# First embedding gate: the norm's root is made by token and spread by a diagonal product, and two sums into the stream run on GpSimd

## The chip, the cores and the metric

The kernel runs on one core of one Trainium2 chip. A core has TensorE (PE, with its weight loads as PEld), VectorE (DVE), ScalarE (ACT), GpSimd (POOL) and SyncE (SP), which here issues the DMAs of the weights. The metric is the device time of one execution in microseconds; the median of three runs of the kernel before is 1048.97 us (1047.62 to 1049.02).

## The reference, cut to what matters

Two decoder layers run over 256 tokens of width 1024 in float32. Each layer is a half-step SwiGLU, a token mixer, a second half-step SwiGLU, and a gated input embedding:

```
for i in range(2):
    h = h + 0.5 * swiglu(rms_norm(h, g_ffn1[i]), ...)
    h = h + mixer_i(rms_norm(h, g_mix[i]), ...)
    h = h + 0.5 * swiglu(rms_norm(h, g_ffn2[i]), ...)
    gate = sigmoid(rms_norm(h, g_ple[i]) @ ple_w_gate[i])
    h = h + gate * (p[i] @ ple_w_proj[i])
# rms_norm(x, g) = x * rsqrt(mean(x * x) + 1e-6) * g
```

The change touches the last two lines of layer 0 only. Layer 1 has a gate of its own (`ple_last`), which is left as it is.

## The kernel before, in words

The residual stream `h` is kept transposed in SBUF: 128 partitions by 8 blocks of the width by 256 tokens. A norm is split in two. `Norm.chunk(dp)` takes two blocks of `h` as soon as they are final: ACT writes the high part of h times the gain (L374), DVE the low part (L376), ACT the squares (L382), and GpSimd adds the squares up (L384) and folds them to `ss` at the fourth chunk (L388). The factor of each token, one over the root of its mean square, is applied behind the matrix product that the norm feeds. A float32 weight is used as two parts: ACT casts the high part `whi` (L86), DVE subtracts it for the low part `wlo` (L87); each block of weights needs three products (L234 to L236), or a wide one and a narrow one (L255, L248) in the feed-forward.

In the gate of layer 0 (`ple`), PE first makes the projection of p (two PSUM tiles of two banks each), then the gate's product in four steps `dp`, each of 48 products into one PSUM tile of the pool `psb`, which has four buffers. After the first half of step 0 the function calls `norm.spread()` (L1087): a product of `ss` with a constant matrix (L394) sums over the partitions and leaves the mean of each token on all 128 partitions, 128x256; DVE adds epsilon (L396) and takes the inverse root in ten instructions of 128x256 (`rsqrt`, L354 and three times L356 to L358). Each step then has its tail: DVE multiplies the gate by `r`, ACT takes the sigmoid (L1090), DVE multiplies by the projection and adds the result into `h` (the instructions of DVE are all recorded under the helper's line, L349), and `after.chunk(dp)` makes the two blocks of input for the next layer's first feed-forward.

That feed-forward (`ffn`) starts with the blocks of width 0 to 5 of the gate and the up product (the wide products of a unit of weights first, then its narrow ones), then blocks 6 and 7; so its fifth block, the first of chunk 2, is needed after eight wide products.

The order on each engine is set by the framework's planner: it lists instructions by their place in the program and puts the first one that its own timing calls ready into the engine's queue. The engine then runs that queue strictly in order. `order(...)` and `steady(...)` pin an instruction behind its engine's previous one of the program while they are switched on; in `ple` both are off, in the feed-forward `steady` is on. SP's weight loads are pinned always.

Two forms that the change brings to this place exist elsewhere in the kernel: `by_token` (L401), where `ss` is the stationary operand and one column of the constant matrix the moving one, so that the means stand on the partitions, 128x2, and a spread by a diagonal matrix in the opening of the kernel (`roots`, L1181 to L1195).

Of the kernel before, what the change touches and what calls it, by code (L numbers as in the profile page):

```python
# [9 lines left out]
F32 = mybir.dt.float32  # L10
# [3 lines left out]
ALU = mybir.AluOpType  # L14
AX = mybir.AxisListType

P = 128
S = 256
# [133 lines left out]
def trunk(ctx: ExitStack, tc: tile.TileContext, a: dict, out: bass.AP):  # L152
    nc = tc.nc
# [4 lines left out]
    stat = ctx.enter_context(tc.tile_pool(name="stat", bufs=2))  # L158
# [5 lines left out]
    def pa():  # L164
        return psa.tile([P, 1024], F32, name="pa", tag="pa")

    def pb():
        return psb.tile([P, 512], F32, name="pb", tag="pb")
# [62 lines left out]
    def mm_w(ps, wt, cols, x, k, start, stop):  # L231

        hi, lo = wt[0][:, cols], wt[1][:, cols]
        steady(nc.tensor.matmul(ps, lhsT=hi, rhs=x[:, k, 0, :], start=start, stop=False, skip_group_check=True))  # L234
        steady(nc.tensor.matmul(ps, lhsT=hi, rhs=x[:, k, 1, :], start=False, stop=False, skip_group_check=True))  # L235
        return steady(nc.tensor.matmul(ps, lhsT=lo, rhs=x[:, k, 0, :], start=False, stop=stop, skip_group_check=True))  # L236
# [32 lines left out]
    start = ExitStack()  # L269
# [40 lines left out]
    ident = const.tile([P, P], F32, name="ident")  # L310
# [3 lines left out]
    ones = const.tile([P, P], F32, name="ones")  # L314
# [33 lines left out]
    def tt_op(o, x, y, op):  # L348
        return nc.vector.tensor_tensor(o, x, y, op=op)  # L349

    def rsqrt(x, n, o):

        t = stat.tile([P, n], F32, name=f"rs_t{n}", tag=f"rs_t{n}", bufs=1)
        order(nc.vector.tensor_scalar(o.bitcast(I32), x.bitcast(I32), -0.5, 1597463007.0, op0=ALU.mult, op1=ALU.add))  # L354
        for _ in range(3):
            order(nc.vector.scalar_tensor_tensor(t, o, -0.5, o, op0=ALU.mult, op1=ALU.mult))  # L356
            order(nc.vector.tensor_tensor(t, t, x, op=ALU.mult))
            order(nc.vector.scalar_tensor_tensor(o, t, 1.5, o, op0=ALU.add, op1=ALU.mult))  # L358

    h = const.tile([P, KD, S], F32, name="h")  # L360

    class Norm:
# [38 lines left out]
        def by_token(self):  # L401

            ss = self.ss
            ms = pb()
            for tt in range(2):
                nc.tensor.matmul(
                    ms[:, tt : tt + 1], lhsT=ss[:, tt * P : (tt + 1) * P], rhs=mean_d[:, 0:1], start=True, stop=True
                )
            x = stat.tile([P, 2], F32, name="mst", tag="mst", bufs=1)
            nc.vector.tensor_scalar(x, ms[:, :2], EPS, None, op0=ALU.add)  # L410
            return x

    def two(r):
        return r.unsqueeze(1).broadcast_to([P, 2, S])
# [652 lines left out]
    def ple(norm, pt, after, pool):  # L1067
        x = norm.x
        wt = w.get()
        pr = []  # L1070
        for q in range(2):
            ps = pa().rearrange("p (b t) -> p b t", b=4)
            for b in range(4):
                for k in range(2):
                    c = (4 * q + b) * P
                    mm_w(ps[:, b, :], wt(k), slice(c, c + P), pt, k, start=(b % 2 == 0 and k == 0), stop=(k == 1))
            pr.append(ps)
        r = None
        for dp in range(4):
            wt = w.get()  # L1080
            gp = pb().rearrange("p (b t) -> p b t", b=2)
            for kh in range(2):
                for b in range(2):
                    for k in range(kh * 4, kh * 4 + 4):
                        mm_w(gp[:, b, :], wt(k), slice(b * P, (b + 1) * P), x, k, start=(k == 0 and b == 0), stop=(k == KD - 1))
                if r is None:
                    r = norm.spread()  # L1087
            gt = pool.tile([P, 2, S], F32, name="gt", tag="gt")
            tt_op(gt, gp, two(r), ALU.mult)
            nc.scalar.activation(gt, gt, AF.Sigmoid)  # L1090
            tt_op(gt, gt, pr[dp // 2][:, 2 * (dp % 2) : 2 * (dp % 2) + 2, :], ALU.mult)
            tt_op(h[:, 2 * dp : 2 * dp + 2, :], h[:, 2 * dp : 2 * dp + 2, :], gt, ALU.add)
            after.chunk(dp)

    def ple_last(norm, pt, pool):
# [44 lines left out]
    norm = Norm(0, 0)  # L1140
# [14 lines left out]
    sums, mean, rt = (const.tile([P, 2], F32, name=n) for n in ("row_sums", "row_mean", "row_r"))  # L1155
# [64 lines left out]
    for i in range(2):  # L1220
        nxt = Norm(1, i)
        with tc.tile_pool(name=f"ffn1_{i}", bufs=2, reuse_waits="tile") as pool:
            if i == 0:
                ffn(norm, nxt, pool, {0: lambda *_: small_loads(), 4: lambda *marks: later(pool, *marks)}, opened)
            else:
                ffn(norm, nxt, pool)
        norm = nxt
        with tc.tile_pool(name=f"mix_{i}", bufs=2, reuse_waits="tile") as pool:
            lazy = Lazy(Norm, 2, i)
            (mla if i == 0 else fox)(norm, lazy, pool)  # L1230
            norm = lazy.norm
        pt = p_parts(i)
        nxt = Norm(3, i)
        with tc.tile_pool(name=f"ffn2_{i}", bufs=2, reuse_waits="tile") as pool:
            ffn(norm, nxt, pool)
            norm = nxt
            if i == 0:
                lazy = Lazy(Norm, 0, 1)
                ple(norm, pt, lazy, pool)
                norm = lazy.norm  # L1240
            else:
                ple_last(norm, pt, pool)
# [41 lines left out]
```

## Time and profile before

| | |
|---|---|
| median of three runs | 1048.97 us (1047.62 to 1049.02) |
| the profiled execution | 1049.13 us |
| its span in the profile | 1047.4 us (1.7 us lie around it) |
| mean granted clock of TensorE | 0.997 of full speed |
| PE, DVE, ACT, POOL busy | 99%, 74%, 57%, 7% of the span |

The profile gives for each engine the time in which it was busy, and for each wait the instruction that released it. A clock of 1.00 means 2.4 GHz, of 0.50 means 1.2 GHz. The gate of layer 0 lies from 489 us (the projection) over 494.6 us (the gate's first product) to 518.1 us (the next feed-forward's first product). Times "at" a moment are counted from the start of the span.

### The profile page before, as it was taken

The page shows a single profiled execution, that of the slowest core. Times are in us where ns is not written, and L with a number is a line of the kernel's source. Part 1 is how long each engine was busy: PE and PEld are TensorE (multiplying, and loading weights), DVE is VectorE, ACT ScalarE, POOL GpSimd, SP SyncE. Part 2 cuts the span into 40 slices and gives each one's busy share as a digit, 9 for nine tenths or more (in the row PEclk, how much of TensorE's full clock was granted, in tenths as well). Part 3 has the DMA queues.
Part 4 walks back from the last instruction along what each step waited for, and adds up shares of the span by engine and source line. Part 5 has one row for each costly group of instructions (what it writes and reads, how often), then busy time and mean ns, then how long its engine had stood idle before and what let it go on. Part 6 is the DMA issues. An engine that isn't in the chain of part 4 may idle for free.

```text
span 1047.4 us, 16326 instructions
## 1 busy us (share of the span) xinstructions
PE 1034.1 (99%) x6380; PEld 918.5 (88%) x6380; DVE 777.6 (74%) x1369; ACT 600.0 (57%) x903; POOL 77.9 (7%) x99
## 2 busy tenths in 40 slices
PE   8999999999999999999999999999999999999998
PEld 7888888987898888889888888889998988888886
DVE  5888766679979776666987776658888797776664
ACT  6665544568766655455656555535655666554552
POOL 0000000233110000001110000011000200000010
PEclk9999999999999999999999999999999999999999
DMA  7765555524336656556537565554743267555541
GB/s 243 242 226 183 185 181 172 181 93 170 106 107 201 214 188 191 183 185 206 170 126 240 188 201 174 188 154 141 227 135 113 95 197 227 182 185 191 181 161 41
DMA packets 171105, 182.60 MB, mean 174 GB/s; under 512 B 6094, under 2 KB 164372, under 8 KB 171028
## 3 DMA queue, kind: packets, MB, share of 16 engines
q1 hardware_dynamic: 170452, 181.03, 53.7%
q8 instruction: 50, 0.82, 0.3%
q10 hardware_dynamic: 576, 0.53, 0.1%
q14 instruction: 27, 0.22, 0.1%
HBM read 180.50 MB, written 1.05 MB: 173 GB/s over the span
## 4 chain that ended last, share of the span: by engine, by line
PE 94%; DVE 3%; DMA 1%; POOL 1%; ACT 0%; issue 0%; ACTq 0%; DVEq 0%
PE pa L255 46%; PE pa L248 23%; PE pa L264 3%; PE pa L266 3%; PE pa L265 3%; PE pa L234 2%; PE pa L236 2%; PE pa L235 2%; DVE wlo L87 1%; PE pb L612 1%; PE pb L519 1%; PE pb L559 1%; PE pb L547 1%; PE pb L518 1%; DMA xn<-in_x_dram 1%; PE pb L266 1%
## 5 line engine op out<-in xcount | busy, mean ns | idle before, releaser
L87 DVE TENSOR_TENSOR wlo<-raw,whi 128x1024 fp32r<-128x1024 f32 (+2 forms) x351 | 418.5, 1223 | 170.9 <-PE pa L248 71.9
L86 ACT CAST whi<-raw 128x1024 fp32r<-128x1024 f32 (+2 forms) x351 | 351.0, 1016 | 247.0 <-PE pa L255 175.9
L255 PE MATMUL pa<-xa,whi 128*128 128x512 f32 x1408 | 343.9, 395 | 1.9 <-DVE xa L376 1.8
L255 PEld LDWEIGHTS pa<-xa,whi 128*128 128x128 f32 x1408 | 258.7, 189 | 54.1 <-DVE xa L376 3.1
L248 PEld LDWEIGHTS pa<-xa,wlo 128*128 128x128 f32 x1408 | 179.1, 189 | 8.7
L248 PE MATMUL pa<-xa,wlo 128*128 128x256 f32 x1408 | 180.6, 279 | 0.0
L255 PE MATMUL pa<-hid,whi 128*128 128x512 f32 x704 | 169.2, 392 | 0.0
L255 PEld LDWEIGHTS pa<-hid,whi 128*128 128x128 f32 x704 | 128.8, 188 | 25.2
L384 POOL TENSOR_TENSOR sq<-sq 128x512 f32<-128x512 f32 x21 | 37.8, 1800 | 826.9 <-ACT sq L382 813.4
L248 PEld LDWEIGHTS pa<-hid,wlo 128*128 128x128 f32 x704 | 88.3, 188 | 4.0
L248 PE MATMUL pa<-hid,wlo 128*128 128x256 f32 x704 | 89.1, 278 | 0.0
L264 PE MATMUL pa<-whi,xa 128*128 128x256 f32 (+3 forms) x192 | 59.0, 307 | 0.0
L266 PE MATMUL pa<-whi,xa 128*128 128x256 f32 (+3 forms) x192 | 57.6, 300 | 0.0
L265 PE MATMUL pa<-wlo,xa 128*128 128x256 f32 (+3 forms) x192 | 57.2, 298 | 0.0
L234 PE MATMUL pa<-xa,whi 128*128 128x256 f32 x184 | 54.2, 295 | 0.0
L349 DVE TENSOR_TENSOR hid<-hf,hid 128x512 fp32r<-128x512 f32 x44 | 30.4, 692 | 29.0 <-ACT hid L442 29.0
L236 PE MATMUL pa<-xa,wlo 128*128 128x256 f32 x184 | 51.9, 283 | 0.0
L235 PE MATMUL pa<-xa,whi 128*128 128x256 f32 x184 | 51.9, 282 | 0.0
L432 ACT COPY gt<-pa 128x512 f32<-128x512 f32 x44 | 25.8, 586 | 39.1 <-PE pa L248 39.0
L432 ACT COPY hf<-pa 128x512 f32<-128x512 f32 x44 | 25.7, 584 | 28.1 <-PE pa L248 28.1
L438 ACT ACTIVATE gt<-gt 128x512 f32<-128x512 f32 x44 | 27.7, 629 | 19.4 <-DVE gt L349 19.3
L264 PEld LDWEIGHTS pa<-whi,xa 128*128 128x128 f32 x192 | 36.1, 188 | 1.4 <-issue 0.5
(281 smaller groups left out, 1215.1 us busy)
## 6 DMA issues: line engine op xcount, KB each, us to landing
raw<-in_ffn_w_in_dram SPq DMA_DIRECT2D x86, 1024.0 KB, 5.1
raw<-in_ffn_w_out_dram SPq DMA_DIRECT2D x32, 1024.0 KB, 5.2
raw<-in_ffn_w_out_dram SPq DMA_DIRECT2D x16, 768.0 KB, 4.5
raw<-in_ple_w_gate_dram SPq DMA_DIRECT2D x8, 1024.0 KB, 5.8
raw<-in_fox_w_in_dram SPq DMA_DIRECT2D x8, 1024.0 KB, 6.5
raw<-in_mla_w_o_dram SPq DMA_DIRECT2D x4, 1024.0 KB, 5.6
raw<-in_fox_w_o_dram SPq DMA_DIRECT2D x4, 1024.0 KB
raw<-in_mla_w_in_dram SPq DMA_DIRECT2D x3, 1024.0 KB, 6.7
```

The costliest lines, as they stand in the source:

```text
L86: self.order(self.nc.scalar.copy(h, whole))
L87: self.order(self.nc.vector.tensor_tensor(low, whole, h.bitcast(F32), op=ALU.subtract))
L234: steady(nc.tensor.matmul(ps, lhsT=hi, rhs=x[:, k, 0, :], start=start, stop=False, skip_group_check=True))
L235: steady(nc.tensor.matmul(ps, lhsT=hi, rhs=x[:, k, 1, :], start=False, stop=False, skip_group_check=True))
L236: return steady(nc.tensor.matmul(ps, lhsT=lo, rhs=x[:, k, 0, :], start=False, stop=stop, skip_group_check=True))
L248: nc.tensor.matmul(ps[:, 1, :], lhsT=wt(k)[1][:, cols], rhs=x[:, at + k, 0, :], start=False, stop=(k == last), skip_group_check=True,)
L255: nc.tensor.matmul(ps, lhsT=wt(k)[0][:, cols], rhs=x[:, at + k], start=(k == first), stop=False, skip_group_check=True)
L264: steady(nc.tensor.matmul(ps, lhsT=x[:, k, 0, t], rhs=wt[0], start=start, stop=False, skip_group_check=True))
L265: steady(nc.tensor.matmul(ps, lhsT=x[:, k, 0, t], rhs=wt[1], start=False, stop=False, skip_group_check=True))
L266: steady(nc.tensor.matmul(ps, lhsT=x[:, k, 1, t], rhs=wt[0], start=False, stop=stop, skip_group_check=True))
L384: nc.gpsimd.tensor_tensor(sq, sq, self.acc, op=ALU.add)
L432: nc.scalar.copy(o, ps[:, :, 0, :])
```

## The change

`spread_small` takes the place of `spread` in the gate of layer 0. It takes the means by token, the root on 128x2, puts the two columns of roots on the diagonal of two 128x128 matrices, and multiplies a matrix of ones with them, which leaves on all 128 partitions the factor of each token; ACT copies it out of PSUM. Beside that, the sums into `h` of steps 0 and 1 are issued on GpSimd instead of DVE.

```diff
+        def spread_small(self):
+
+            x = self.by_token()
+            rt = stat.tile([P, 2], F32, name="rt", tag="rt", bufs=1)
+            rsqrt(x, 2, rt)
+            diag = stat.tile([P, S], F32, name="ms", tag="ms", bufs=1)
+            for tt in range(2):
+                nc.vector.tensor_scalar(diag[:, tt * P : (tt + 1) * P], ident, rt[:, tt : tt + 1], None, op0=ALU.mult)
+            rp = pb()
+            nc.tensor.matmul(rp[:, :S], lhsT=ones, rhs=diag, start=True, stop=True)
+            r = stat.tile([P, S], F32, name="r", tag="r")
+            nc.scalar.copy(r, rp[:, :S])
+            return r
...
                 if r is None:
-                    r = norm.spread()
+                    r = norm.spread_small()
...
-            tt_op(h[:, 2 * dp : 2 * dp + 2, :], h[:, 2 * dp : 2 * dp + 2, :], gt, ALU.add)
+            hc = h[:, 2 * dp : 2 * dp + 2, :]
+            if dp < 2:
+                nc.gpsimd.tensor_tensor(hc, hc, gt, op=ALU.add)
+            else:
+                tt_op(hc, hc, gt, ALU.add)
```

## Rows read from the trace of the kernel before

**Rows 1.** The page, part 1: busy time, share and instructions of each engine.
```profile
PE 1034.1 (99%) x6380; PEld 918.5 (88%) x6380; DVE 777.6 (74%) x1369; ACT 600.0 (57%) x903; POOL 77.9 (7%) x99
```
**Rows 2.** Waits of PE in the whole span: us in total, times, longest.
```profile
PE pa L255 <- DVE xa L376: 1.8, 1, 1.8
...
PE pb L406 <- POOL ss L388: 1.2, 1, 1.2
...
PE pb L394 <- POOL ss L388: 0.3, 1, 0.3
```
**Rows 3.** Windows: PE, PEld, DVE, ACT, POOL busy; then granted clock, DMA share, GB/s.
```profile
498.00:507.00 9.00, 9.00 (x76) 8.95 (x76) 8.72 (x16) 2.63 (x4) 0.00 (x0) 1.00 0.57 180
507.00:514.00 7.00, 7.00 (x61) 7.00 (x61) 6.21 (x10) 6.47 (x10) 0.00 (x0) 1.00 0.68 220
514.00:522.00 8.00, 6.16 (x46) 5.47 (x44) 8.00 (x13) 6.32 (x11) 1.69 (x2) 1.00 0.41 132
522.00:530.00 8.00, 8.00 (x39) 7.11 (x40) 5.54 (x7) 3.27 (x5) 4.35 (x3) 0.79 0.41 132
```
**Rows 4.** Timeline of PE through the gate: start, us, instructions, idle before and releaser.
```profile
497.81 0.70 PE L394 MATMUL pb<-ss,mean_d 128*128 128x256 f32 x2 [0.34 <-POOL ss L388]
498.16 0.47 PE L234 MATMUL pb<-xa,whi 128*128 128x256 f32 x1
...
518.14 2.00 PE L255 MATMUL pa<-xa,whi 128*128 128x512 f32 x8
521.98 1.93 PE L255 MATMUL pa<-xa,whi 128*128 128x512 f32 x4 [1.84 <-DVE xa L376]
```
**Rows 5.** Timeline of DVE through the gate.
```profile
498.77 0.41 DVE L396 TENSOR_SCALAR ms<-pb 128x256 f32<-128x256 f32 x1
...
502.73 1.22 DVE L87 TENSOR_TENSOR wlo<-raw,whi 128x1024 fp32r<-128x1024 f32 x1
...
505.23 0.42 DVE L358 SCALAR_TENSOR_TENSOR r<-rs_t,r 128x256 f32<-128x256 f32 x1
...
510.00 1.28 DVE L349 TENSOR_TENSOR gt<-gt,pa 128x512 f32<-128x512 f32 x2 [0.72 <-ACT gt L1090]
...
515.13 0.68 DVE L349 TENSOR_TENSOR gt<-pb,r 128x512 f32<-128x512 f32 x1
...
521.45 0.87 DVE L376 SCALAR_TENSOR_TENSOR xa<-h,gvec,xa 128x256 fp32r<-128x256 f32 x2
```
**Rows 6.** Timeline of DVE in the opening: first and last of thirteen instructions in a row.
```profile
24.73 0.16 DVE L1184 TENSOR_SCALAR row_mean<-row_sums 128x2 f32<-128x2 f32 x1
...
26.96 0.48 DVE L1189 TENSOR_SCALAR ms<-ident,row_r 128x128 f32<-128x128 f32 x2
```
**Rows 7.** Timeline of PE in the opening and in the first mixer.
```profile
28.45 0.59 PE L1192 MATMUL pb<-ms,ones 128*128 128x256 f32 x2
...
209.11 0.50 PE L406 MATMUL pb<-mean_d,ss 128*128 128x1 f32 x4
...
210.22 0.50 PE L264 MATMUL pa<-whi,zt 128*128 128x512 f32 x1
...
213.08 0.28 PE L234 MATMUL pa<-xa,whi 128*128 128x256 f32 x1
```
**Rows 8.** ACT by shape: the copies of 128x256 out of PSUM nearest to the new one.
```profile
L568 ACT CAST xa<-pb 128x256 fp32r<-128x256 f32 x16 | 5.9, 369 | 10.7 <-PE pb L564 10.5
```
**Rows 9.** Timeline of ACT in the gate's first step.
```profile
504.13 1.05 ACT L86 CAST whi<-raw 128x1024 fp32r<-128x1024 f32 x1 [1.76 <-PE pb L235]
```
**Rows 10.** Instructions on the gate's tile: the sums into h, ns min/median/max.
```profile
L349 DVE TENSOR_TENSOR h<-h,gt x4: 673/683/1066, 511.2 to 523.0; 128x512 f32<-128x512 f32 x4
```
**Rows 11.** Timeline of POOL near 308 us: sums of 128x512.
```profile
307.68 2.21 POOL L384 TENSOR_TENSOR sq<-sq 128x512 f32<-128x512 f32 x1 [32.59 <-ACT sq L382]
310.64 1.30 POOL L384 TENSOR_TENSOR sq<-sq 128x512 f32<-128x512 f32 x1 [0.74 <-ACT sq L382]
```
**Rows 12.** Timeline of DVE beside the first of these.
```profile
308.65 1.92 DVE L376 SCALAR_TENSOR_TENSOR xa<-h,gvec,xa 128x256 fp32r<-128x256 f32 x2
```

## The prediction

> **What bounds the kernel now.** I read the page's first part, then the waits of TensorE, then its timeline and the windows round the one place those waits name. PE is busy 99% of the span [rows 1], so only time in which PE stands still or runs slowly can be won. The waits of PE name few places, and the longest lies in the stretch of this change: 1.8 us in which the next feed-forward's products wait for DVE's low part of the input [rows 2]. On the timeline the feed-forward starts at 518.14, runs eight wide products, idles 1.84 us, and goes on at 521.98 [rows 4]: it could have gone on at 521.98 - 1.84 = 520.14. The ninth product needs the first block of chunk 2, whose low part DVE makes at 521.45 [rows 5].
>
> The idle time has a price behind it. In the eight us after it the granted clock is 0.79, while in the three windows before it is 1.00 [rows 3]: PE is at its lower level of 1.2 GHz for part of them, and (1 - 0.79) x 8 = 1.68 us of work is lost. Stall and clock together cost 1.84 + 1.68 = 3.52 us. This is all that the change can win here.
>
> DVE makes the stall. It is busy 8.72 of 9 us, 6.21 of 7 and 8.00 of 8 up to 522 [rows 3]. From 498.16 to 518.14 PE makes 24 + 3 x 48 = 168 gate products [rows 4], 0.119 us each, so step 3 takes 5.7 us and step 2's tile is full at about 512.7 (518.14 - 5.7, and 0.3 until the last one lands: estimates from these rows). DVE begins on it at 515.13 [rows 5], 2.4 us late: a backlog that began with the root.
>
> **The change part by part.** *The root.* It goes from 498.77 to 505.23 + 0.42 = 505.65, with two weight subtractions (L87) of 1.22 us inside, of which one is shown [rows 5]: 6.88 - 2.44 = 4.44 us of DVE. In its place come the epsilon, the ten of the root and two diagonals, thirteen instructions. The opening has the same thirteen without a gap, 24.73 to 26.96 + 0.48 = 27.44, so 2.71 us [rows 6]. DVE wins 4.44 - 2.71 = 1.73 us.
>
> *The means.* Four products with one column in place of two of 128x256: 0.50 us against 0.70 [rows 7, 4]. Both wait for the same fold on GpSimd (0.34 us of idle, rows 4), which stays. I put this at nothing.
>
> *The diagonal product* is new on PE. The same shape took 0.59 us in the opening [rows 7]; in the gate the next product began 0.35 us after a pair of that shape [rows 4]. Between 0.35 and 0.59 I take 0.35, since it stands among the same neighbours.
>
> *Its wait.* PE runs in order, so if the planner puts this product too early, the gate products behind it wait, and DVE, ACT and the casts that need their buffers wait for those. Bounds: nothing, or the whole chain from means to diagonals (the rival below). The planner does put other work ahead of a product that isn't ready: in the first mixer the products L264, written after those of L234, ran at 210.22, ahead of them at 213.08 [rows 7]. Where its timing errs, PE has waited 0.3 and 1.2 us [rows 2]. I take 0.4, near the smaller.
>
> *The copy* on ACT, 128x256 out of PSUM: 0.37 us by the nearest row [rows 8], at most 1.05 + 0.37 if it stands behind a cast that itself waits for PE [rows 9]. So r comes at 498.77 + 2.71 + two L87 of 1.22 + 0.59 + 0.37 = 504.9, or near 506 behind that cast, against 505.65 before. The factor comes hardly sooner; what is won is DVE's time, which the weight subtractions fill while PE and ACT make it.
>
> *The two sums.* They take 2 x 0.683 = 1.37 us off DVE [rows 10] and put two of 1.30 to 2.21 us on GpSimd [rows 11], which is idle from 498 to 514 [rows 3]. Behind them there waits the sum of squares of chunk 1, and on ACT the scaling of chunks 0 and 1 with the casts behind it. Each of these chunks may come 0.6 to 1.5 us later; PE doesn't ask for them before 518.14, and DVE had finished both by 515.13, so this is covered, up to 3 us.
>
> A sum on GpSimd is not free for DVE. Beside the one of 2.21 us a pair of L376 took 1.92 us, against 0.87 in the gate [rows 11, 12, 5]: DVE was held 1.05 us. Two sums hold it between 0 (as far as DVE has nothing to do just then) and 2.10 us. I take 1.4, as DVE is busy nearly throughout. The Trainium skill ("SBUF — State Buffer", section "Who interferes with whom") has a rule that speaks against the move: a DVE instruction with two SBUF inputs and a GpSimd one that reads SBUF shut each other out for a whole instruction. By it the two sums would cost DVE their full length, 2.6 us, and the move would lose more than it saves; the row's 1.05 us lies a little under that.
>
> *Sum for DVE:* 1.73 + 1.37 - 1.4 = 1.7 us, and up to 0.72 more if the wait for the sigmoid at 510.00 [rows 5] goes. The low part of chunk 2's first block, ready at 521.98, then comes at about 520.3, between 519.6 (the whole 2.4 us of backlog gone, which is as far as any relief can reach) and 521.0 (2.10 held).
>
> *Sum for PE:* the ninth product is reached at 520.14 + 0.35 + 0.4 = 520.89. The later of the two counts, 520.89. So 521.98 - 520.89 = 1.09 us of the stall is won, and without idle time there the clock stays at 2.4 GHz: 1.68 us. Together 2.77 us. Chunk 3 is asked for after sixteen more wide products and all the narrow ones, and its tail starts no later than before; the feed-forward behind is bound by PE and keeps what is won. From the profiled execution's 1049.13 us (span 1047.4) that gives 1046.36 us; this execution lies 0.16 us above the median of the runs, so **1046.2 us** is predicted.
>
> **The rivals.** *A, the forecast:* 1045.8 (no wait at the diagonal product, 3.52 - 0.35 = 3.17 us won) to 1047.0 (a wait of 1.2 us, which leaves 0.29 + 1.68 us won). Chance 0.56, a tenth of it not beyond the bound of measurement.
>
> *B, DVE is not relieved enough.* By the whole-instruction rule the relief is 1.73 + 1.37 - 2.6 = 0.5 us, the block comes at 521.5 and PE still idles 0.6 us: 1046.8 if the clock holds, 1048.5 if it falls again; with no relief at all the old stall stays, 1049.0. For it: DVE is busy 8.00 of 8 us before 522 [rows 3], and the factor comes hardly sooner. Against it: the row beside a sum shows less than a full length held, and DVE has 0.8 us of slack from 507 to 514, where the sums would run. The skill's page named above would make this the outcome. Chance 0.24, a sixth of it faster than the bound.
>
> *C, slower: the diagonal product in PE's queue right behind the means.* Then PE waits for the thirteen instructions and one L87, 2.71 + 1.22 = 3.9 us, and the clock, which 1.84 us of idle brought down, falls again (1.68): 3.9 + 0.35 + 1.68 - 3.52 = 2.4 us slower, 1051.4. It decides from 1.5 us of waiting on, where wait, product and clock make up the 3.52 us won. For it: it stands there in the program, and the means do run at their place in the program [rows 4]. Against it: the products that overtake in rows 7. Chance 0.10, nine tenths of it slower than the bound.
>
> *D, the planner orders later work otherwise*, since its clock reads otherwise from here on, and casts or attention tails move a little: 1.5 us either way on top of A, 1045 to 1051. Nothing in the rows speaks for it but that it can. Chance 0.10: 0.03 faster, 0.04 the same, 0.03 slower.
>
> **How the numbers follow.** About 0.2%, 2.1 us, is what a measurement of this kernel can tell from no change: below 1046.87 is faster, above 1051.07 slower. Faster: 0.50 (A) + 0.04 (B) + 0.03 (D) = 0.57. Slower: 0.09 (C) + 0.03 (D) = 0.12. The same: 0.31. The range takes all of A, B except a stall that stays whole, and half of D, 0.8 in all: 1045.1 to 1049.3. A alone is 1045.8 to 1047.0.
>
> **What would show it.** Right: the wait of the feed-forward's wide products for L376 is gone or under 0.5 us, the windows after 518 are at a clock of 1.00, thirteen short instructions stand on DVE after 498.8, PE waits under 1 us for the diagonal product, and step 2's multiply starts within 1 us of its last product. Wrong: PE idle at the diagonal product for over 1.5 us (C); DVE instructions beside the two sums on GpSimd stretched by over 1.05 us each and the stall still there (B); the gate as forecast, but PE waits elsewhere that were not there (D).

## The result, and the profile after

The changed kernel takes 1053.85 us (median of four runs, 1053.29 to 1054.19) against 1048.30 for the kernel before on the same chip: a ratio of 1.0059 with an interval of 1.0046 to 1.0071. It is slower, by 5.6 us in the medians and 6.2 by the ratio. Faster was forecast, 1046.2 us; the time lies outside the range too. A few executions, of the kernel before too, took 1.2 to 5.9 ms; they are left out of every ratio and count below. The profiled execution took 1054.19 us, with a span of 1052.5 and a mean granted clock of 0.999.

Part 1 of the page of the kernel after, which answers to [rows 1]:

```profile
PE 1039.8 (99%) x6384; PEld 918.7 (87%) x6384; DVE 774.8 (74%) x1369; ACT 600.1 (57%) x904; POOL 79.8 (8%) x101
```

The span grew by 5.1 us, and PE's busy time by 1039.8 - 1034.1 = 5.7 us, with four products more. A lower clock would lengthen the busy time too, but the mean clock is 0.999 after and 0.997 before. So PE doesn't wait longer in sum; it works longer on the same products. That already speaks against every rival of the prediction, all of which look for the time in waits, in the clock behind them or in the order.

The waits of PE in the kernel after (us in total, times, longest), which answer to [rows 2]:

```profile
PE pb L406 <- POOL ss L388: 1.2, 1, 1.2
PE pb L422 <- DVE ms L420: 1.1, 1, 1.1
```

The wait of 1.8 us for the low part of chunk 2 is no longer in the list, as forecast; there is a new one of 1.1 us for the diagonals. The windows round the gate of the kernel after (columns as in [rows 3]):

```profile
498.00:507.00 9.00, 7.77 (x63) 7.31 (x62) 8.28 (x18) 4.46 (x6) 2.26 (x2) 1.00 0.46 151
507.00:514.00 7.00, 7.00 (x63) 7.00 (x62) 5.09 (x7) 5.14 (x8) 1.30 (x1) 1.00 0.45 150
514.00:522.00 8.00, 8.00 (x71) 8.00 (x70) 7.22 (x9) 5.81 (x9) 2.71 (x2) 1.00 0.50 164
522.00:530.00 8.00, 8.00 (x47) 6.91 (x46) 6.66 (x10) 5.83 (x9) 3.15 (x3) 1.00 0.70 231
```

PE is busy throughout from 507 on and the clock of the last window is 1.00, where it was 0.79. PE's timeline in the kernel after, which answers to [rows 4]:

```profile
500.39 0.61 PE L406 MATMUL pb<-mean_d,ss 128*128 128x1 f32 x4
...
503.63 0.28 PE L236 MATMUL pb<-xa,wlo 128*128 128x256 f32 x1
505.05 0.70 PE L422 MATMUL pb<-ms,ones 128*128 128x256 f32 x2 [1.14 <-DVE ms L420]
505.39 0.47 PE L234 MATMUL pb<-xa,whi 128*128 128x256 f32 x1
505.70 0.28 PE L235 MATMUL pb<-xa,whi 128*128 128x256 f32 x1
...
522.39 2.96 PE L255 MATMUL pa<-xa,whi 128*128 128x512 f32 x12
```

The product of the means starts at 500.39; before it started at 497.81 [rows 4]. The kernel is 2.58 us late before the change has done anything in the gate. To compare the gate itself, 2.58 is taken off below. DVE's timeline in the kernel after, which answers to [rows 5]:

```profile
501.35 0.15 DVE L410 TENSOR_SCALAR mst<-pb 128x2 f32<-128x2 f32 x1
...
502.40 1.22 DVE L87 TENSOR_TENSOR wlo<-raw,whi 128x1024 fp32r<-128x1024 f32 x1
...
504.51 0.48 DVE L420 TENSOR_SCALAR ms<-ident,rt 128x128 f32<-128x128 f32 x2
...
509.60 1.68 DVE L87 TENSOR_TENSOR wlo<-raw,whi 128x1024 fp32r<-128x1024 f32 x1 [0.78 <-ACT whi L86]
...
515.20 1.71 DVE L87 TENSOR_TENSOR wlo<-raw,whi 128x1024 fp32r<-128x1024 f32 x1 [0.74 <-ACT whi L86]
...
517.63 0.68 DVE L349 TENSOR_TENSOR gt<-pb,r 128x512 f32<-128x512 f32 x1
...
522.32 0.88 DVE L376 SCALAR_TENSOR_TENSOR xa<-h,gvec,xa 128x256 fp32r<-128x256 f32 x2
```

And the two sums on GpSimd in the kernel after:

```profile
508.90 1.30 POOL L1108 TENSOR_TENSOR h<-h,gt 128x512 f32<-128x512 f32 x1 [8.56 <-DVE gt L349]
514.54 1.29 POOL L1108 TENSOR_TENSOR h<-h,gt 128x512 f32<-128x512 f32 x1 [4.33 <-DVE gt L349]
```

**Where the time came from.** Apart from the gate's own new products, PE runs the same products in the same order in both kernels. What differs is their pace, and only in some lines. Instructions of line L255 in the kernel before (ns min/median/max of one, first and last start):

```profile
L255 PE MATMUL pa<-xa,whi x1408: 388/392/774, 8.8 to 949.4; 128*128 128x512 f32 x176
...
L255 PE MATMUL pa<-hid,whi x704: 388/392/397, 134.2 to 1010.4; 128*128 128x512 f32 x176
```

The same of the kernel after:

```profile
L255 PE MATMUL pa<-xa,whi x1408: 389/396/774, 8.9 to 954.4; 128*128 128x512 f32 x176
...
L255 PE MATMUL pa<-hid,whi x704: 387/392/399, 135.3 to 1015.5; 128*128 128x512 f32 x176
```

The 1408 wide products that read `xa` are 4 ns longer in the median; the 704 that read `hid`, with weights from the same buffers, are not. The lengths are modelled, so I took the starts. PE's timeline of a steady group in the kernel before:

```profile
61.98 3.84 PE L255 MATMUL pa<-xa,whi 128*128 128x512 f32 x16
65.65 1.98 PE L248 MATMUL pa<-xa,wlo 128*128 128x256 f32 x16
```

The same group in the kernel after:

```profile
62.15 3.89 PE L255 MATMUL pa<-xa,whi 128*128 128x512 f32 x16
65.88 2.03 PE L248 MATMUL pa<-xa,wlo 128*128 128x256 f32 x16
```

Sixteen wide products take 65.65 - 61.98 = 3.67 us before and 65.88 - 62.15 = 3.73 us after: 229 against 233 ns from one start to the next. Taken from all starts of the trace, the wide ones on `xa` go from 229.3 to 233.3 ns or a little more (1408 of them: 5.6 us and up), the narrow ones (L248) from 115.7 to 116.7 ns (1408 x 1.0 = 1.4 us), and those on `hid` stay or gain up to 0.6 ns. That is about 7 us lost over the whole span. The clock is 1.00 on both sides of it.

What these products have in common is an address. The change declares one new tile, `rt`, of 8 bytes per partition, which takes a slot of 32 bytes in the pool `stat`. The pools are laid out one behind the other, `act` (with `xa`) ahead of `stat`, and the weights and `hid` behind it. In the compiled programs `xa` stays at 31232 and 47616, `whi` moves from 108224 to 108256, `wlo` from 132800 to 132832, `hid` from 158208 to 158240. The distance of the moving operand `xa` from the weights (its address less theirs, modulo 256) goes from 64 to 32 bytes; that of `hid` from the weights stays. My theory is that this distance sets the pace. The rivals: the change's work at the gate, and through it the planner's order, costs the time; or the absolute address of a tile does.

### The profile page after: what moved, and what is told of

Read it like the earlier page. It is cut to its first block, busy times and chain, and to the rows that moved or that the text cites. A ratio compares the mean times of both kernels' runs of the same rounds, so it can differ in the third digit from the quotient of the medians.

```text
span 1052.5 us, 16337 instructions
## 1 busy us (share of the span) xinstructions
PE 1039.8 (99%) x6384; PEld 918.7 (87%) x6384; DVE 774.8 (74%) x1369; ACT 600.1 (57%) x904; POOL 79.8 (8%) x101
## 4 chain that ended last, share of the span: by engine, by line
PE 95%; DVE 3%; DMA 1%; issue 0%; ACT 0%; POOL 0%; ACTq 0%; DVEq 0%
PE pa L255 47%; PE pa L248 23%; PE pa L264 3%; PE pa L266 3%; PE pa L265 3%; PE pa L234 2%; PE pa L236 2%; PE pa L235 2%; PE pb L626 1%; PE pb L533 1%; PE pb L573 1%; DVE wlo L87 1%; PE pb L561 1%; PE pb L532 1%; DMA xn<-in_x_dram 1%; PE pb L236 1%
## 5 line engine op out<-in xcount | busy, mean ns | idle before, releaser
L87 DVE TENSOR_TENSOR wlo<-raw,whi 128x1024 fp32r<-128x1024 f32 (+2 forms) x351 | 419.4, 1225 | 176.6 <-PE pa L248 76.5
L255 PE MATMUL pa<-xa,whi 128*128 128x512 f32 x1408 | 347.9, 397 | 0.0
L255 PEld LDWEIGHTS pa<-xa,whi 128*128 128x128 f32 x1408 | 257.9, 188 | 56.9 <-DVE xa L376 0.8
L248 PEld LDWEIGHTS pa<-xa,wlo 128*128 128x128 f32 x1408 | 179.0, 188 | 9.3
L248 PE MATMUL pa<-xa,wlo 128*128 128x256 f32 x1408 | 180.9, 279 | 0.0
L255 PE MATMUL pa<-hid,whi 128*128 128x512 f32 x704 | 169.1, 392 | 0.0
L255 PEld LDWEIGHTS pa<-hid,whi 128*128 128x128 f32 x704 | 128.7, 188 | 25.1
L248 PEld LDWEIGHTS pa<-hid,wlo 128*128 128x128 f32 x704 | 87.9, 188 | 4.1
L248 PE MATMUL pa<-hid,wlo 128*128 128x256 f32 x704 | 88.7, 277 | 0.0
```

Source lines behind the costliest of these rows:

```text
L87: self.order(self.nc.vector.tensor_tensor(low, whole, h.bitcast(F32), op=ALU.subtract))
L248: nc.tensor.matmul(ps[:, 1, :], lhsT=wt(k)[1][:, cols], rhs=x[:, at + k, 0, :], start=False, stop=(k == last), skip_group_check=True,)
L255: nc.tensor.matmul(ps, lhsT=wt(k)[0][:, cols], rhs=x[:, at + k], start=(k == first), stop=False, skip_group_check=True)
```

## The experiments

**The slot alone.** The kernel before, with an unread tile of the same size in `stat` and nothing else.

```diff
     def ple(...):
+        stat.tile([P, 2], F32, name="pad", tag="pad", bufs=1)
```

> The kernel before, with one tile of 8 bytes (a slot of 32) that nothing reads put at the end of the statistics pool, where the change puts its tile of roots. No instruction differs; raw, the weight parts and all that lies behind stand 32 bytes further, xa stays. Theory 'placement' (the weights' place against xa sets the pace of the products that read xa): as slow as the changed kernel in all but the gate, 1055 us, some 7 us over before; L255 on xa at 0.233 us a product against 0.229, on hid unchanged. Rival 'work' (the change's own instructions cost the 5.5 us): 1048.3 us, the same as before.

Measured: 1055.82 us against 1047.25, a ratio of 1.0071 (1.0058 to 1.0084). No instruction differs from the kernel before. The same steady group in this kernel's PE timeline:

```profile
61.70 3.89 PE L255 MATMUL pa<-xa,whi 128*128 128x512 f32 x16
65.43 2.03 PE L248 MATMUL pa<-xa,wlo 128*128 128x256 f32 x16
...
524.01 1.94 PE L255 MATMUL pa<-xa,whi 128*128 128x512 f32 x4 [1.92 <-DVE xa L376]
```

3.73 us for sixteen, as in the changed kernel, and the old stall at the gate is still there. So the placement alone costs all of the loss and a little more; the gate's new work isn't its cause.

**The change without the slot.** The root lies in a buffer that exists already.

```diff
-            rt = stat.tile([P, 2], F32, name="rt", tag="rt", bufs=1)
+            rt = stat.tile([P, S], F32, name="r", tag="r")[:, :2]
```

> The whole change, but the two roots by token stand in a free buffer of the tag r instead of a tile of their own, so that nothing is moved; the order on every engine is that of the changed kernel. 'Placement': 2.1 us faster than before, 1046.2 us, since the trace of the changed kernel gains 2.1 us in the gate. 'Work': 1053.8 us as the changed kernel.

Measured: 1046.99 us against 1047.25, 0.9995 (0.9986 to 1.0004). The 7 us are gone, and the order of every engine is that of the changed kernel. With the run before this shows the cause from both sides. It also gives the first measurement of the gate by itself: no difference that could be told from none, where 2.1 us less was expected.

**Distance or address?** The kernel before with the same unread 32 bytes ahead of `xa`, so that `xa` and the weights move together.

```diff
+    const.tile([P, 2], F32, name="cpad")
```

> The kernel before with the unread tile of 32 bytes in the constant pool, ahead of xa: xa, the weight parts and hid all stand 32 bytes further, and the distances between them are those of before. 'Placement by distance': 1048.3 us, as before. 'Placement by address' (the weights must not stand off a multiple of 64): about 1055 us, and hid's products slow too. 'Work': 1048.3 us, so this run speaks only between the first two.

Measured: 1048.79 us against 1047.25, 1.0015 (1.0006 to 1.0024); the wide products on `xa` run at 229.2 to 229.9 ns. Every address has moved and the pace has stayed: it is the distance. A rest of 1.5 us is not explained; in this kernel's profile the old stall at the gate is 2.3 us, 0.4 more than before.

**Sixty-four bytes.** The kernel before with a pad of 16 words, which brings the distance to 0 modulo 256.

```diff
+        stat.tile([P, 16], F32, name="pad", tag="pad", bufs=1)
```

> The kernel before with an unread tile of 64 bytes at the end of the statistics pool: raw, weight parts and hid stand 64 bytes further, xa stays. If the pace hangs on whether the distance between weights and xa is a multiple of 64 bytes: as before, 1047 to 1048 us, L255 on xa at 0.229 us. If any step from the place of before is slow: 1055 us and 0.233 us.

Measured: 1053.38 us against 1047.18, 1.0054 (1.0041 to 1.0068). The expectation was missed. The wide products on `xa` of line L255 in this kernel:

```profile
L255 PE MATMUL pa<-xa,whi x1408: 387/389/776, 8.9 to 954.7; 128*128 128x512 f32 x176
```

The narrow ones of line L248 in it:

```profile
L248 PE MATMUL pa<-xa,wlo x1408: 274/283/415, 10.8 to 956.7; 128*128 128x256 f32 x176
```

The wide products did become a little faster (392 to 389 ns; 228.5 to 229.2 from start to start, 0.8 less), the narrow ones slower (115.7 to 119.5 from start to start): 1408 x (3.8 - 0.8) = 4.2 us of the 5.6 that the ratio gives. Wide and narrow products have different good distances, which my theory had not held.

**The pace by itself.** 36 groups of 32 wide products behind one that isn't counted, the moving operand 32 bytes further on in each group, no other engine at work.

```diff
+            c = i // 2 % 4 * 512 + off
+                nc.tensor.matmul(ps, lhsT=wts[:, i % 8 * P : (i % 8 + 1) * P], rhs=mov[:, c : c + 512], start=True, stop=True)
+    for j in range(36):
+        group(("even", "odd")[j % 2], 8 * j)
```

> None of the reference's work: 37 groups of 32 products 128x128 by 128x512 in the weights' type, nothing else running; the moving operand starts 32 bytes further in each group, the weights stay. If the distance of the two operands alone sets the pace: even groups (multiples of 64 bytes) 32 x 0.229 = 7.34 us, odd groups 32 x 0.2335 = 7.47 us, in turn. If it takes the other engines' traffic: all groups alike.

PE's timeline in this probe; each line is one group:

```profile
20.42 7.42 PE L59 MATMUL even<-mov,wts 128*128 128x512 f32 x32
27.67 7.63 PE L59 MATMUL odd<-mov,wts 128*128 128x512 f32 x32
35.14 7.50 PE L59 MATMUL even<-mov,wts 128*128 128x512 f32 x32
42.48 7.64 PE L59 MATMUL odd<-mov,wts 128*128 128x512 f32 x32
49.95 7.63 PE L59 MATMUL even<-mov,wts 128*128 128x512 f32 x32
...
79.84 7.44 PE L59 MATMUL even<-mov,wts 128*128 128x512 f32 x32
87.12 3.20 PE L59 MATMUL odd<-mov,wts 128*128 128x512 f32 x13
```

From start to start the groups take 7.25, 7.47, 7.34, 7.47 us; after eight groups, 256 bytes, the first figure is back (87.12 - 79.84 = 7.28). Per product that is 226.6 ns at 0, 229.4 at 64 and 233.4 at 32 and, within 1 ns, at all other steps. 229 and 233 are the paces of the kernel before and after, whose distances are 64 and 32. No other engine takes part, so it is no contention with one. The probe moves one operand only; that the distance counts and not that operand's own address is shown by the run in which both moved. The Trainium skill ("TensorE: Matmul & The Clock Gate", "Back-to-back issue gap") gives some 216 ns for 512 columns at the full clock as the gap of an isolated product and 131 ns for a sustained stream, both from the columns alone; here the same shape took 226.6 to 233.4 in a stream, by where it lay, so the measurement decides.

**Narrow products.** The same probe with 18 wide and 18 narrow groups.

```diff
+    for n in (512, 256):
+        for j in range(18):
+            group(("even", "odd")[j % 2], 8 * j, n)
```

> None of the reference's work: the groups of 32 products again, the moving operand 32 bytes further in each, 18 groups of 512 columns and 18 of 256. Wide: the pattern of the first probe again, repeating after eight groups (256 bytes): 7.27 us at 0, 7.34 at 64, 7.47 at the others. Narrow, if the same rule holds with half the columns: 3.64, 3.67, 3.73 us. If narrow products have another order of places: another pattern, since with a distance of 0 they took 0.1195 us in the kernel moved by 64 bytes against 0.1155 before.

PE's timeline of this probe, the first two groups of 256 columns and three later ones:

```profile
154.12 4.00 PE L59 MATMUL even<-mov,wts 128*128 128x256 f32 x32
157.96 3.94 PE L59 MATMUL odd<-mov,wts 128*128 128x256 f32 x32
...
176.88 3.81 PE L59 MATMUL even<-mov,wts 128*128 128x256 f32 x32
180.53 3.94 PE L59 MATMUL odd<-mov,wts 128*128 128x256 f32 x32
184.31 4.00 PE L59 MATMUL even<-mov,wts 128*128 128x256 f32 x32
```

3.84 us at 0, 3.77 at 32 and 64, 3.65 at 192, 3.78 at 224, and 3.84 again at 256: 120.0 ns at the worst, 114.1 at the best. The narrow products have the period of the wide ones and another order of places: 0, the best for the wide, is the worst for the narrow, as in the run with 64 bytes (119.5). At 64 and 32, the distances of the kernels before and after, the probe shows one pace for them, 117.8 ns, where the kernels had 115.7 and 116.7. So the probe accounts for the wide products' 5.6 us; what sets the narrow ones apart in the kernels, 1.4 us, it doesn't show.

**Placing each part by itself.** A pad of 64 bytes, and a gap of 192 bytes between the weights' high and low parts, so that `whi` lies at distance 0 and `wlo` at 64.

```diff
+                if u == 0 and k0 == 0:
+                    self.split.tile([P, 48], F32, name="gap", tag="gap", bufs=1)
...
+        stat.tile([P, 16], F32, name="pad", tag="pad", bufs=1)
```

> The kernel before, no instruction changed; an unread tile of 64 bytes ahead of the weights puts whi at a distance of 0 modulo 256 bytes from xa (and hid), another of 192 bytes between whi and wlo leaves wlo at 64 as before. If the distance sets the pace: L255 at 0.227 us in place of 0.229, so 2112 x 0.0023 = 5 us less, 1042 to 1043 us, and narrow products as before. If only the narrow ones' loss of the run moved by 64 bytes counted: no gain, 1047 us.

Measured: 1053.97 us against 1047.77, 1.0070 (1.0055 to 1.0085). A miss: wide products 231 ns in the mean, narrow ones 117.8. In a steady group the first ten wide products take between 224 and 240 ns and only the last six 226 to 227, the probe's pace at 0. `xa` and `whi` stand at the very addresses of the run with 64 bytes, where the wide products took 228.5 in the mean. So the distance of each part to `xa` alone doesn't give the pace of the whole kernel; what else counts (the place of the two parts to each other, and so what ran just before, is one candidate) stays open.

**The change, a whole period further.** The tile of the roots made 256 bytes long: everything behind it moves by 256.

```diff
-            rt = stat.tile([P, 2], F32, name="rt", tag="rt", bufs=1)
+            rt = stat.tile([P, 64], F32, name="rt", tag="rt", bufs=1)[:, :2]
```

> The whole change as it is, order and instructions the same, but its tile of roots takes 256 bytes instead of a slot of 32, so that raw, weight parts and hid stand 256 bytes further than before. If the pace repeats after 256 bytes, as in the probes: L255 on xa back at 0.229 us and the time of the whole change without moved tiles, 0.9995 of before, about 1047 us. If any move off the place of before costs: 1054 us as the changed kernel.

Measured: 1046.68 us against 1048.04, 0.9988 (0.9979 to 0.9997), with the instructions of the changed kernel in the same order. A steady group in its PE timeline:

```profile
72.27 3.83 PE L255 MATMUL pa<-xa,whi 128*128 128x512 f32 x16
75.94 2.04 PE L248 MATMUL pa<-xa,wlo 128*128 128x256 f32 x16
```

3.67 us for sixteen, the pace of before. The period holds in the kernel. This version is faster than the changed kernel, and by 1.3 us than the one before (0.3 to 2.2); that last step rests on this run, since the run without the slot, with the same work in the same order and at the same pace, gave 0.9995 (0.9986 to 1.0004).

**The sums alone.** The kernel before with only the two sums moved to GpSimd.

```diff
-            tt_op(h[:, 2 * dp : 2 * dp + 2, :], h[:, 2 * dp : 2 * dp + 2, :], gt, ALU.add)
+            if dp < 2:
+                nc.gpsimd.tensor_tensor(hc, hc, gt, op=ALU.add)
+            else:
+                tt_op(hc, hc, gt, ALU.add)
```

> The kernel before with the sums of steps 0 and 1 on GpSimd and the root as before; nothing is moved in memory. If DVE is relieved: up to 1.4 us of the 1.84 us stall go, 1046 to 1047 us. If GpSimd holds DVE for as long as it saves (1.05 us a sum): the stall stays, 1047.3 us, the same as before.

Measured: 1050.68 us against 1047.18, 1.0027 (1.0018 to 1.0036): slower. GpSimd's timeline in this kernel:

```profile
510.34 3.53 POOL L1108 TENSOR_TENSOR h<-h,gt 128x512 f32<-128x512 f32 x2 [13.00 <-DVE gt L349]
...
521.74 1.33 POOL L384 TENSOR_TENSOR sq<-sq 128x512 f32<-128x512 f32 x1 [4.96 <-ACT sq L382]
```

DVE's timeline in it:

```profile
511.04 1.68 DVE L87 TENSOR_TENSOR wlo<-raw,whi 128x1024 fp32r<-128x1024 f32 x1 [0.18 <-ACT whi L86]
512.64 2.70 DVE L376 SCALAR_TENSOR_TENSOR xa<-h,gvec,xa 128x256 fp32r<-128x256 f32 x4
...
521.86 1.89 DVE L376 SCALAR_TENSOR_TENSOR xa<-h,gvec,xa 128x256 fp32r<-128x256 f32 x2
```

DVE's four L376 at this place in the kernel before:

```profile
513.54 1.67 DVE L376 SCALAR_TENSOR_TENSOR xa<-h,gvec,xa 128x256 fp32r<-128x256 f32 x4
```

PE's timeline in the kernel with the sums alone:

```profile
517.72 2.00 PE L255 MATMUL pa<-xa,whi 128*128 128x512 f32 x8
523.40 1.85 PE L255 MATMUL pa<-xa,whi 128*128 128x512 f32 x4 [3.69 <-DVE xa L376]
```

The stall has doubled, 3.69 us for 1.84. The two sums run together at 510.34, stretch the L87 beside them by 1.68 - 1.22 = 0.46 us and the four L376 by 2.70 - 1.67 = 1.03, and chunk 2's own pair of L376 now meets a sum of squares at 521.74 and takes 1.89 us for 0.87. Without the shorter root the move costs DVE 0.46 + 1.03 + 1.02 = 2.5 us, more than the 1.37 us it takes off it. The rule of the Trainium skill that the prediction weighed ("SBUF — State Buffer", "Who interferes with whom") agrees with the outcome: the pair at 521.86 was held 1.02 us beside an instruction of 1.33, though the L87 and the four L376 together only 1.49 beside 3.53.

**The root alone.** The change without the slot and with all sums left on DVE.

```diff
-            r = norm.spread()
+            r = norm.spread_small()    # rt in the buffer of r, sums on DVE
```

> The kernel before with the root by token and the diagonal product (roots in a free buffer, nothing moved), the four sums into h all on DVE. If the sums on GpSimd cost and the root wins: below the whole change without the moved tiles (0.9995 of before), about 1046 us or 0.999, with the stall before the ninth product gone. If the root's gain is eaten by PE's wait for the diagonal: 1.000.

Measured: 1047.69 us against 1047.77, 0.9996 (0.9987 to 1.0005). The stall is gone with the root alone (0.4 us remain, for the gate's tile), the wait of 1.1 us for the diagonals is there. The sums on GpSimd add nothing to it that could be told from none.

**The wait for the diagonals.** The change without the slot, with the diagonal product pinned twelve gate products later and step 0's tail behind it; run twice, the second time for its trace.

```diff
+                tc.keep_in_program_order(nc.tensor.matmul(rp[:, :S], lhsT=ones, rhs=diag, start=True, stop=True))
...
+                    if dp == 1 and r is None:
+                        r = finish()
+                        tail(0, first)
```

> As the run without the moved tiles, and the diagonal product pinned twelve gate products later, with the tail of step 0 written behind it. If PE's 1.1 us wait for the diagonal is the planner's misplacement: that wait goes, 1.1 us under the run without moved tiles, 1045.1 us. If what is behind it becomes late instead (step 0's tail, the chunks of the next feed-forward): no gain, 1046.2 us, and PE waits for xa again.

> The run with the diagonal product twelve gate products later once more, for its trace. If the wait for the diagonal is gone, PE should show no wait above 0.3 us there; the 1.1 us that did not come out of the time then shows as a wait in another place of the gate or the next feed-forward (a chunk of xa, a buffer of PSUM). If the wait is still there, twelve products were not enough: 1047.0 us as without the pin.

Measured: 1047.19 us against 1047.25, 0.9997 (0.9988 to 1.0006), and 1047.33 against 1047.18, 0.9998 (0.9989 to 1.0007). PE's timeline of the second:

```profile
519.61 1.20 PE L255 MATMUL pa<-xa,whi 128*128 128x512 f32 x4 [0.46 <-DVE xa L376]
...
522.85 3.03 PE L255 MATMUL pa<-xa,whi 128*128 128x512 f32 x12 [0.68 <-DVE gt L349]
```

PE no longer waits for the diagonals, but the tail comes later, and the 1.14 us come back as 0.46 + 0.68 = 1.14 at the feed-forward. The wait only changed its place.

## Why the prediction was wrong

**The step that failed** is the sum for PE: "Together 2.77 us", taken whole off the span because "the feed-forward behind is bound by PE and keeps what is won". It takes for granted that PE's other products go on at the pace of the kernel before: a term put at nothing without a reason. The prediction counted every instruction of the change and not its new tile. `rt` costs about 7 us by its 32 bytes, about twice all that the gate could win ("This is all that the change can win here", 3.52 us). None of the rivals had it; D, "orders later work otherwise", came nearest, since it looked for time outside the gate, but with up to 1.5 us either way, behind the gate alone and by another order: the loss begins ahead of the gate (2.58 us by then), and PE's order didn't change.

**The gate, step by step**, in the profiled executions, with 2.58 us taken off the times of after.

- DVE's relief: the number is right, the sum behind it only in part. The root runs from 501.35 to 504.51 + 0.48 = 504.99, with one L87 of 1.22 inside: 2.42 us of its own, forecast 2.71. Chunk 2's block comes at 522.32 + 0.53 (from start to release, as in rows 5 and 4) - 2.58 = 520.27; forecast 520.3. That it fits to 0.1 us is partly luck. Between the root's start and chunk 2's first L376 one L87 (8 before, 7 after) and step 3's multiply have moved behind, some 1.8 us that the forecast didn't have, and DVE stands idle for 3.2 us where it was 1.1, which it didn't have either.
- The sums beside it: the L87 at 509.60 and 515.20 took 1.68 and 1.71 us for 1.22, so DVE was held about 0.95 us; forecast 1.4. Step 2's multiply at 517.63 is no longer 2.4 us late, since its tile is full at 522.39 - 5.6 + 0.3 = 517.1 by the prediction's own working. But it starts hardly sooner, 517.63 - 2.58 = 515.05 against 515.13: it is the tile that is full later, by 1.8 us, for the most part by PE's wait and the new product.
- The product itself: right. The next one starts 505.39 - 505.05 = 0.34 us later, forecast 0.35; the one behind it is late as well (0.31 for 0.12).
- Its wait: too low. 1.14 us, forecast 0.4 within bounds of 0 to 3.9. From 503.63 to 505.70 two product steps of 0.12 became 2.07 us: 1.83 us for wait and product, forecast 0.75. The means, put at nothing, gave 0.23 back (1.27 us around L394 in the starts before, 1.04 around L406).
- The ninth product: 522.39 + 8 x 0.233 - 2.58 = 521.67, forecast 520.89. So 0.31 us of the stall is won and not 1.09; the mechanism held, wait and product took the rest.
- The clock: 1.00 behind the gate, as forecast, 1.68 us. In this pair of executions the gate gives 0.31 + 1.68 = 2.0 us, forecast 2.77.

Span by span: 7.1 lost by pace - 2.0 won at the gate = 5.1 us, which is 1052.5 - 1047.4. The 7.1 is the rest of this sum; the paces give about 7.

**Over many executions** the gate gave less: 0.9995 and 0.9988 without the shift of distance, whose intervals share a gain of 0.3 to 1.5 us. One reason is shown: the 1.68 us of clock were taken as certain. They would raise the mean clock of an execution by 1.68 / 1047 = 0.0016, but it was 0.9976 over 27 executions of the kernel before and 0.9974 over the 11 of the run without the slot, and 0.9973 (15) and 0.9978 (11) in the pair of the last version: a third of it at best. Nor did the stall always bring the clock down: the run with 64 bytes had a stall of 1.61 us and no fall behind it. Window of that kernel:

```profile
522.00:530.00 8.00, 6.39 (x34) 5.20 (x33) 7.77 (x11) 5.47 (x10) 2.95 (x2) 1.00 0.74 250
```

In the other profiles with the stall (before, the two pads of 32 bytes, the sums alone, the placed parts) the clock did fall behind it. And a fall of the same kind stands in the first 20 us of some profiles (0.88 in the first ten of the last version) and not of others, whatever the kernel; in the profiles of both versions without the shift one stands there, and none at the gate. What brings it there is not settled. It is part of the spread of 4 us between executions, in which a gain of 1 us is hard to see.

## What to carry to other kernels

Where PE is busy 99% of the time, read its busy time over the same products before its waits: a small change of pace, 4 ns in 230, outweighs every stall in the list. A tile of 8 bytes in an early pool moves all that lies behind it; put small tiles into buffers that exist, or give them the period's 256 bytes, and compare the addresses of the operands of the busiest products before an effect is put down to the edit itself. And price a wait added to PE together with the stall it removes: here one took the place of the other to within 0.3 us.

## What the runs showed of the hardware

- TensorE's pace on these float32 products depends on the distance of its two operands in SBUF, with a period of 256 bytes: 226.6, 229.4 or some 233.4 ns for 512 columns, 114.1 to 120.0 ns for 256, at a granted clock of 1.00 and with no other engine running.
- The good distances of wide and narrow products differ (0 is the best for one, the worst for the other), so a layout that is best for both parts of a weight can't be read from one of them; in the whole kernel two layouts with `whi` at distance 0, the best place of the wide products, were 0.5% and 0.7% slower. The probe gives the kernels' pace for wide products at 64 and 32 bytes, but not for narrow ones.
- Two instructions that hold each other up can be moved apart or together by a third: the sums on GpSimd ran together and cost 0.27% with the long root; with the short one they ran apart (508.90 and 514.54) and cost nothing that could be told from none.
